# Seven-product pairs in every matrix stage from the output projection to the end of a decoder layer

## The chip, the cores and the metric

The kernel runs on one core of a Trainium2 chip. The metric is the device time of one execution in microseconds; the time of a kernel is the median of its runs. A profile of one execution goes with it; its times count from the first instruction.

## What is computed

One layer of a decoder trunk for 256 tokens of width 2048, all in float32:

```python
h = rmsnorm(x, norm_mix_g)
proj = h @ w_in + b_in                       # 2048 -> 9216, split in six
merged = sigmoid(g_conv) * conformer_conv(u_conv) + sigmoid(g_att) * (moba(q, k, v) @ w_att_out)
x = x + merged @ w_out                       # 2048 -> 2048
h, m = rmsnorm(x, norm_cross_g), rmsnorm(mem, norm_mem_g)
x = x + cross_attention(h, m, w_cq, w_ckv, w_co)   # 4 heads of 512, 256 memory tokens
h = rmsnorm(x, norm_ffn_g)
g, u = split(h @ w_ffn_in)                   # 2048 -> 2 x 5632
x = x + (silu(g) * u) @ w_ffn_out            # 5632 -> 2048
return rmsnorm(x, norm_final_g)
```

The matrices make up nearly all the work: 315 MB of float32 weights, each read once.

## The kernel before

**Products.** Full float32 precision comes from splitting both sides in a high part (a cast to fp32r) and a low part (the rest). A *product* (`mm3`, L214) multiplies a 128 x 128 piece of the left side (features by tokens, stationary) by a 128 x 512 piece of weights in three matmuls: high by high (L217), high by low (L218), low by high (L219). ScalarE makes the high part of the weights, VectorE subtracts it from the raw weights to get the low part; both are recorded under L78, the line of the helper that passes on every operation.

**Blocks.** `stream` (L564) runs a list of blocks, one for each 1024 columns of output and all features: nine for `w_in` (glu, k, q, v, gates), ao0/ao1 and co0/co1 (attention and convolution out), wo0/wo1 (output projection), cq0/1, ck0/1, cv0/1, xo0/1 (cross attention), ffn0 to ffn10 and fo0/fo1. A block has four outputs (token half t, column half n), each in a PSUM bank. Features are taken in pairs of 128. A pair has a kind:

- K: two units of weights of 128 rows each, 128 x 1024 casts; 8 products.
- W: one unit of 256 rows, 128 x 2048 casts; 8 products.
- S: the 2 x 2 product of 128-blocks in seven products (`pair_s`, L507; tables `OF_RAW`, `OF_SUMS`). VectorE makes four sums of the raw weights; unit "a" holds three raw quarters, unit "b" the four sums, and each is cast and subtracted. The left side needs four sums (*forms*) beside its four quarters. The seven products accumulate in their own banks over all S pairs of a block (p1 to p7, with c22 eight in all, the W pairs adding to p2, p3, p4 and c22); `sums_early` (L539) and `result` (L555) put them together with eight adds.

Only ffn1 to ffn10 have S pairs, three of eight (`S_PAIRS`, L1026), and W pairs beside them. All other blocks, ffn0, fo0 and fo1 included, are K. A block of K or W pairs has 64 products (32 in ao and co, 176 in fo), an ffn block with three S pairs 61.

**Order.** The order of the instructions on each engine is written by the program as it is built. In K blocks `advance` (L445) casts and subtracts up to `AHEAD` units before they are used. For W and S units `pump` (L462) does it after each product, when an estimated clock of VectorE or ScalarE is less than `LEAD` ahead of TensorE's (a product counts as 0.68 us). Raw weights land in a ring of half-units (places for 128 rows), high and low parts in another: four places each, ten from `room_for_sums` (L634) in ffn0 on. All weights come by SyncE's (SP's) DMA queue.

Everything else (transposes of a result, the split of the next left side, normalization, attention) is put at a slot so many ticks after the block's evacuation (`at`, L165). Transposes (four 128 x 128 ones in a bank) go to one of two PSUM banks set apart ("misc"); six are for accumulators.

**Left sides.** Each stage has its own 2 MB + 2 MB of high and low parts in SBUF (mg, x2, m, ca, x3, mid); x stays in SBUF until ffn0, where `park_x` writes it to DRAM. The results of the ffn blocks ("mid", 5632 x 256) are transposed and parked in DRAM by ScalarE's queue (L1243). fo0 reloads them pair by pair on SP's queue (`mid_load`, L1257), splits them (`mid_split`, L1263) and keeps all of them for fo1.

Of the kernel before, what the change touches and what calls it, by code (L numbers as in the profile page):

```python
# [37 lines left out]
class Block:  # L38
# [6 lines left out]
    def __init__(self, name, kt, lhs, cols, evac, before=None, kinds=None, forms=None):  # L45
        self.name, self.kt, self.lhs, self.cols, self.evac = name, kt, lhs, cols, evac
        self.before, self.kinds, self.forms = before, kinds or "K" * (kt // 2), forms
# [14 lines left out]
class Timed:  # L62
# [7 lines left out]
    def __getattr__(self, name):  # L70
# [9 lines left out]
        return call  # L80

# [48 lines left out]
class Builder:  # L130
    AHEAD = 6
    LEAD = 0.7

    def __init__(self, ctx, tc, args):
# [16 lines left out]
        self.acc = e(tc.tile_pool(name="acc", bufs=6, space=PSUM))  # L151
        self.misc = e(tc.tile_pool(name="misc", bufs=2, space=PSUM))
# [8 lines left out]
        self.after_sums = []  # L161
# [3 lines left out]
    def at(self, delay, fn, *args):  # L165
        heapq.heappush(self.tasks, (self.slot + delay, self.seq, fn, args))
        self.seq += 1

    def later(self, tr, n):

        for w in range(2):
            self.at(6 + 2 * n + 2 * w, tr, n, w)

    def run_due(self):
        while self.tasks and self.tasks[0][0] <= self.slot:
            _, _, fn, args = heapq.heappop(self.tasks)
            fn(*args)
        self.fill_credit += self.fill_rate
# [4 lines left out]
    def flush(self, upto=None):  # L183
        while self.tasks:
            _, _, fn, args = heapq.heappop(self.tasks)
            fn(*args)
# [21 lines left out]
    def bank(self, shape, name):  # L208
        return self.misc.tile(shape, F32, tag="misc", name=self.nm(name))
# [16 lines left out]
    def transposes(self, src, hi, lo, k, gain=None, mark=None, pool=None):  # L226

        nc = self.nc
        if pool:
            b = pool.tile([P, 2, 2, P], F32, tag="acc", name=self.nm("tr"))  # L230
        else:
            b = self.bank([P, 2, 2, P], "tr")
        for c in range(2):
            for t in range(2):
                nc.tensor.transpose(b[:, c, t, :], src(c, t), self.ident)  # L235
        bb = b.rearrange("p c t s -> p c (t s)")
        if lo is None:
            self.act.copy(hi[:, k : k + 2, :], bb)
        elif gain is None:
            self.split(bb, hi[:, k : k + 2, :], lo[:, k : k + 2, :])  # L240
        else:
            for c in range(2):
                g = self.vecs[:, gain + k + c : gain + k + c + 1]
                self.act.activation(hi[:, k + c, :], bb[:, c, :], AF.Copy, scale=g)
                self.dve.scalar_tensor_tensor(
                    lo[:, k + c, :], bb[:, c, :], g, hi[:, k + c, :].bitcast(F32),
                    op0=ALU.mult, op1=ALU.subtract,
                )
        if mark:
            self.ready.update((mark, k + c) for c in range(2))  # L250

# [18 lines left out]
    def feature_rstd(self, src, first, gap, done):  # L270
# [10 lines left out]
        def total():  # L281
            bk = self.bank([P, 2, 2], "ssq")
# [8 lines left out]
        self.at(first + gap * 7 + 3, total)  # L291

    def rstd_of(self, ss, name):
# [13 lines left out]
        return r  # L307

# [153 lines left out]
    def pump(self):  # L462

        t = self.clock
        while self.n_cast < len(self.units) and self.units[self.n_sub][2] != "K":
            at = self.can_cast()
            if at is not None and max(t["act"], at) < t["pe"] + self.LEAD:
                self.cast_one(at)
                continue
            at = self.can_sub()  # L470
            if at is not None and max(t["dve"], at) < t["pe"] + self.LEAD:
                self.sub_one(at)
                continue
            return

# [4 lines left out]
    def tick(self):  # L480
        self.slot += 1
        self.run_due()

    def acc_of(self, key):
        if key not in self.accs:
            pool = self.misc if key in ("p5", "c22") else self.acc
            self.accs[key] = pool.tile([P, 512], F32, tag="misc" if pool is self.misc else "acc", name=self.nm("acc"))
            self.done[key] = 0
        return self.accs[key]

    def product(self, key, lhs, rhs):
# [6 lines left out]
        t["pe"] += 0.68  # L498
        t["from"] = t["pe"]
        self.pump()  # L500

    def piece(self, blk, k, w, i, t, n):
        lh, ll = blk.lhs(k)
# [3 lines left out]
    def pair_s(self, blk, u, p, first):  # L507

        hi, lo = blk.forms(p)

        self.unit = u

        def go(prods, w):
            for i, (key, left, right) in enumerate(prods):
                f = LEFT[left]
                self.product(key, (hi[:, f, :], lo[:, f, :]), (w[0][:, right, :], w[1][:, right, :]))
# [22 lines left out]
    def sums_early(self):  # L539

        a, dve = self.accs, self.dve
        r = {(t, 1): self.tok_tile([P, 512], "c") for t in range(2)}
        for t in range(2):
            r[t, 0] = self.kept[:, 2 * (self.n_blk % 2) + t]
        self.act.copy(r[0, 0], a["p1"])
        dve.tensor_tensor(r[0, 1], a["p6"], r[0, 0], op=ALU.subtract)
        dve.tensor_tensor(r[1, 0], a["p7"], r[0, 1], op=ALU.add)
        dve.tensor_tensor(r[0, 1], a["p5"], r[0, 1], op=ALU.add)
        dve.tensor_tensor(r[1, 1], a["p5"], r[1, 0], op=ALU.add)
        self.res = r  # L550
        for i, fn in enumerate(self.after_sums):
            self.at(3 + 2 * i, fn)
        self.after_sums = []

    def result(self, blk, t, n):  # L555

# [848 lines left out]
```

## Time and profile before

| | |
|---|---|
| time, median of 3 runs | 1708.89 us (1708.69 to 1710.53) |
| time of the profiled execution | 1708.69 us |
| its span, first to last instruction | 1706.9 us |
| TensorE matmul busy, instructions | 1694.7 us, 7740 |
| VectorE busy | 1186.3 us (70%) |
| ScalarE busy | 854.5 us (50%) |
| GpSimd (POOL) busy | 1.6 us |
| DMA | 346 MB, mean 203 GB/s |

How to read it: matmuls are pipelined, so each is shown longer than the distance between two of them. A row of groups ends with the busy time, the mean of one instruction in ns, the idle time of its engine just before them and who ended it. A row of windows has start and end, the length, and for each engine its busy time and (x) instructions: TensorE's matmuls and weight loads, VectorE (DVE), ScalarE (ACT), GpSimd; then the granted TensorE clock, the busy share of the DMA engines and GB/s.

The blocks that matter start at these times (us): co0 463, wo0 508.5, cq0 599.4, cq1 644.8, ck0 691.1, cv0 782.0, xo0 890.3, ffn0 985.1, ffn1 1030.6, fo0 1455.0, fo1 1576.7.

### The profile page before, as it was taken

Reading aid. Unit: us, or ns where it says so; the run is one execution under the profiler, and the core shown is the slowest. Engines: PE = TensorE matmul, PEld = TensorE weight load, DVE = VectorE, ACT = ScalarE, POOL = GpSimd, SP = SyncE. Lnnn points to the kernel's source line nnn. Section 1 sums busy time; section 2 is a strip of 40 time slices with the busy share of each in tenths; the row PEclk is TensorE's granted clock in tenths of the full one; section 3 lists DMA queues with packets and bytes.
Section 4 is the critical chain, followed back from the end, with each engine's and each line's share of the span. In section 5 each row is a group of like instructions: output and inputs, shape, how many; then the busy total and the mean of one; then the engine's idle time right before and its main releaser. Section 6 shows DMA issues by size and latency. Waiting matters only on the chain.

```text
span 1706.9 us, 20756 instructions
## 1 busy us (share of the span) xinstructions
PE 1694.7 (99%) x7740; PEld 1406.0 (82%) x7740; DVE 1186.3 (70%) x1367; ACT 854.5 (50%) x969; POOL 1.6 (0%) x12
## 2 busy tenths in 40 slices
PE   9999999999999999999999999999999999999998
PEld 7888888888888888888888888888888888888786
DVE  7579987787775566444554569888888887655544
ACT  6444445544544456445444566555555554544433
POOL 0000000000000000000000000000000000000000
PEclk9999999999999999999999999999999999999999
DMA  8665555455666565554355578666666663876653
GB/s 300 197 202 197 198 198 180 158 199 194 209 206 219 186 233 185 185 183 156 131 181 182 184 246 297 213 212 212 211 211 213 210 209 124 315 246 210 194 192 132
DMA packets 129380, 346.00 MB, mean 203 GB/s; under 512 B 14336, under 2 KB 14464, under 8 KB 128896
## 3 DMA queue, kind: packets, MB, share of 16 engines
q1 hardware_dynamic: 125536, 336.12, 59.2%
q10 hardware_dynamic: 3744, 8.56, 1.4%
q8 instruction: 60, 0.98, 0.2%
q14 instruction: 40, 0.33, 0.1%
HBM read 334.67 MB, written 9.96 MB: 202 GB/s over the span
## 4 chain that ended last, share of the span: by engine, by line
PE 98%; ACT 1%; DVE 1%; DMA 0%; issue 0%; ACTq 0%; DVEq 0%
PE acc L218 31%; PE acc L219 31%; PE acc L217 31%; PE tr L235 2%; DVE wlo L78 0%; ACT whi L78 0%; PE cs L219 0%; PE cs L217 0%; PE cb L219 0%; PE cb L218 0%; PE cs L218 0%; PE cb L217 0%; DMA vecs<-in_vecs 0%; PE tr L1048 0%; PE ms L900 0%
## 5 line engine op out<-in xcount | busy, mean ns | idle before, releaser
L78 DVE TENSOR_TENSOR wlo<-raw,whi 128x1024 fp32r<-128x1024 f32 (+2 forms) x474 | 600.2, 1278 | 371.1 <-ACT whi L78 363.8
L78 ACT CAST whi<-raw 128x1024 fp32r<-128x1024 f32 (+2 forms) x474 | 512.8, 1095 | 460.4 <-PE acc L219 362.6
L217 PE MATMUL acc<-whi,xh 128*128 128x512 f32 x576 | 228.9, 397 | 0.7 <-ACT whi L78 0.7
L219 PE MATMUL acc<-whi,xl 128*128 128x512 f32 x576 | 224.6, 390 | 0.0
L218 PE MATMUL acc<-wlo,xh 128*128 128x512 f32 x576 | 224.3, 389 | 0.2 <-DVE wlo L78 0.2
L217 PE MATMUL acc<-whi,x 128*128 128x512 f32 x436 | 171.7, 394 | 0.0
L219 PE MATMUL acc<-whi,x 128*128 128x512 f32 x436 | 170.0, 390 | 0.0
L218 PE MATMUL acc<-wlo,x 128*128 128x512 f32 x436 | 169.8, 389 | 0.0
L217 PE MATMUL acc<-w,x 128*128 128x512 f32 x366 | 143.6, 392 | 0.0
L219 PE MATMUL acc<-w,x 128*128 128x512 f32 x366 | 142.6, 390 | 0.0
L218 PE MATMUL acc<-w,x 128*128 128x512 f32 x366 | 142.5, 389 | 0.0
L218 PE MATMUL acc<-wlo,mid 128*128 128x512 f32 x352 | 137.3, 390 | 1.6 <-DVE wlo L78 1.4
L217 PE MATMUL acc<-whi,mid 128*128 128x512 f32 x352 | 137.3, 390 | 0.1
L219 PE MATMUL acc<-whi,mid 128*128 128x512 f32 x352 | 137.0, 389 | 0.0
L219 PEld LDWEIGHTS acc<-whi,xl 128*128 128x128 f32 x576 | 108.1, 188 | 22.9
L218 PEld LDWEIGHTS acc<-wlo,xh 128*128 128x128 f32 x576 | 108.3, 188 | 22.3 <-DVE wlo L78 0.5
L217 PEld LDWEIGHTS acc<-whi,xh 128*128 128x128 f32 x576 | 108.2, 188 | 22.2 <-ACT whi L78 0.9
L78 DVE TENSOR_TENSOR w<-raw,w 128x2048 fp32r<-128x2048 f32 (+1 forms) x48 | 100.2, 2087 | 16.4 <-DMA raw<-in_w_ffn_in 9.4
L78 DVE SCALAR_TENSOR_TENSOR vy<-vt,vecs,vy 128x256 f32<-128x256 f32 x240 | 104.0, 480 | 0.0
L217 PE MATMUL acc<-whi,m 128*128 128x512 f32 x256 | 101.3, 396 | 0.0
L219 PE MATMUL acc<-whi,m 128*128 128x512 f32 x256 | 99.9, 390 | 0.0
L218 PE MATMUL acc<-wlo,m 128*128 128x512 f32 x256 | 99.7, 390 | 0.0
(219 smaller groups left out, 2476.9 us busy)
## 6 DMA issues: line engine op xcount, KB each, us to landing
raw<-in_w_ffn_in SPq DMA_DIRECT2D x352, 256.0 KB, 4.1
raw<-in_w_in SPq DMA_DIRECT2D x112, 512.0 KB, 4.2
raw<-in_w_ffn_out SPq DMA_DIRECT2D x88, 512.0 KB, 4.7
raw<-in_w_ckv SPq DMA_DIRECT2D x64, 512.0 KB, 3.5
raw<-in_w_in SPq DMA_DIRECT2D x64, 256.0 KB, 4.0
raw<-in_w_out SPq DMA_DIRECT2D x32, 512.0 KB, 4.7
raw<-in_w_cq SPq DMA_DIRECT2D x32, 512.0 KB, 4.6
raw<-in_w_co SPq DMA_DIRECT2D x32, 512.0 KB, 4.0
```

Of the source, the lines that this page charges most:

```text
L78: return f(out, *args, **kwargs)
L217: mm(out, lhs[0], rhs[0], start=start, stop=False)
L218: mm(out, lhs[0], rhs[1], start=False, stop=False)
L219: mm(out, lhs[1], rhs[0], start=False, stop=stop)
L235: nc.tensor.transpose(b[:, c, t, :], src(c, t), self.ident)
```

## The change

1. **S pairs from wo0 on.** Every block from wo0 is made of W and S pairs: two S pairs of eight in wo, cq, ck, cv, xo, ffn0 and ffn1, three in ffn2 to ffn10 as before, six of 22 in fo0 and fo1. ao, co and the blocks before them stay K.
2. **Left sides in shared pieces.** `left_unit` makes one pair's high and low parts, and for an S pair its forms, in 128 x 2048 pieces handed from stage to stage as soon as the last block that reads them has passed (`quad`, `form`, `left_quad_done`). With a gain or an S pair the transposed values are first copied ("a") by ScalarE. As mid's pieces are given back after use, fo1 reloads and splits all of mid again.
3. **Residual in DRAM.** wo and xo load x in 512-column parts into four places ("kept"), add, and write the sum to DRAM; the memory is loaded in eight units through the same places, during cq0 and cq1. These DMAs, mid's stores and reloads go by GpSimd's (POOL's) queue.
4. **Banks by hand.** All eight PSUM banks are one list; accumulators, transposes and attention take whichever was read first.
5. **Work by estimated clocks.** From wo0 on, the pieces of ScalarE's and VectorE's work are tasks with what they depend on and a due time. `pump` emits, after each product and tick, the task or weight operation that can start first (within 0.15 us of it the one due first). Transposes and attention on TensorE wait in a list until what they read is 3 us old by the clocks and a bank is free (`run_aux`).
6. The rings have eight places for parts and six for raw weights from co1 on.

```diff
+                 on_pair=None):
...
-        self.before, self.kinds, self.forms = before, kinds or "K" * (kt // 2), forms
+        self.before, self.last, self.keep, self.on_pair = before, last, keep, on_pair
+        self.kinds = "K" * (kt // 2) if s is None else "".join("WS"[p in s] for p in range(kt // 2))
...
-    LEAD = 0.7
+    LEAD, OLD, PRODUCT = 0.6, 3.0, 0.68
...
-        self.acc = e(tc.tile_pool(name="acc", bufs=6, space=PSUM))
-        self.misc = e(tc.tile_pool(name="misc", bufs=2, space=PSUM))
+        banks = e(tc.tile_pool(name="banks", bufs=1, space=PSUM))
+        self.banks = [banks.tile([P, 512], F32, tag=f"bank{i}", name=f"bank{i}") for i in range(8)]
...
+    def pick(self, eng):
...
+        found = []
+        for x in self.pending[eng]:
+            at = self.start_of(x)
+            if at is not None:
+                found.append((at, x.due, x))
+        if self.n_sub < len(self.units) and self.units[self.n_sub][2] != "K":
+            at = self.can_cast() if eng == "act" else self.can_sub()
+            if at is not None:
+                v = self.n_cast if eng == "act" else self.n_sub
+                due = self.clock["pe"] + (self.products[v] - self.count) * self.PRODUCT - (2.5 if eng == "act" else 0)
+                found.append((max(at, self.clock[eng]), due, self.cast_one if eng == "act" else self.sub_one))
+        if not found:
+            return None
+        first = min(x[0] for x in found)
+        return min((x for x in found if x[0] <= first + 0.15), key=lambda x: x[1])
...
+    def pump(self, until=None):
...
+        until = self.clock["pe"] + self.LEAD if until is None else until
+        while True:
+            found = [x for x in (self.pick(e) for e in ("dve", "act")) if x]
+            if not found:
+                return
+            at, _, x = min(found, key=lambda x: x[0])
+            if at >= until:
+                return
+            if type(x) is Task:
+                self.emit(x)
+            else:
+                x(at)
...
+    def run_aux(self, force=False):
...
+        for i, (fn, deps, when) in enumerate(self.aux):
+            if when and not when():
+                continue
+            if not force:
+                if any(d.done is None or d.done > pe for d in deps):
+                    continue
+                if not any(self.bank_ready(i) <= pe for i in self.free_banks):
+                    return
+            del self.aux[i]
...
+    def left_unit(self, name, p, src, gain=None, at=None):
...
+        first = None
+        if gain is not None or s:
+            first = self.task("act", copy, [], at, due)
+            get = lambda: m["a"]
+        else:
+            get = src
+        high = self.task("act", lambda: act.copy(hi, get()), [first], at, due)
+        low = self.task("dve", lambda: dve.tensor_tensor(lo, get(), hi.bitcast(F32), op=ALU.subtract), [high], at, due)
+        self.marks[name, p] = low
+        if s:
...
+            f = self.task("dve", sums, [first], at, due)
+            h = self.task("act", lambda: act.copy(y[:, 0], m["f"]), [f], at, due)
+            self.marks[name, p, "f"] = self.task(
+                "dve", lambda: dve.tensor_tensor(y[:, 1], m["f"], y[:, 0].bitcast(F32), op=ALU.subtract),
+                [h, low], at, due)
...
-    def room_for_sums(self):
...
+    def more_places(self):
+        for _ in range(2):
+            x = self.big_tile([P, 2, 4, 512], F32R, "w")
+            self.w_ring.add(x[:, 0], x[:, 1])
         x = self.big_tile([P, 8, 512], F32, "raw")
...
+        def load_x(j):
+            for t in range(2):
+                for n in range(2):
+                    c = j * 1024 + n * 512
+                    nc.gpsimd.dma_start(b.kept[:, 2 * t + n], src(t, c))
...
+    S_PAIRS = {"mg": [4, 6], "x2": [4, 6], "m": [5, 6], "ca": [4, 6], "x3": [1, 3, 5], "mid": [3, 6, 9, 12, 15, 18]}
...
+                     S_PAIRS["x3"] if j > 1 else S_PAIRS["x3"][1:], j == 10, True)
...
+    MID_LOADS, MID_SPLITS = 5, 3
...
+    def mid_load(g):
+        p = g % (KF // 2)
+        if g < KF:
+            b.need(b.marks["md", p])
+            m = b.tok_tile([P, 2, S], "mr")
+            nc.gpsimd.dma_start(m, tiles["md"][:, 2 * p : 2 * p + 2, :])
+            mids[g] = m
+    def mid_split(g):
+        j, p = divmod(g, KF // 2)
+        if g < KF:
+            if p == 0:
+                b.left_new(f"mid{j}", S_PAIRS["mid"])
+            m = mids.pop(g)
+            b.left_unit(f"mid{j}", p, lambda: m, None, b.clock["pe"] + 0.5)
...
+        def on_pair(p):
+            g = j * (KF // 2) + p
+            mid_load(g + MID_LOADS)
+            mid_split(g + MID_SPLITS)
...
+        return Block(f"fo{j}", KF, f"mid{j}", [(w, j * 1024), (w, j * 1024 + 512)], evac, before, S_PAIRS["mid"],
+                     True, on_pair=on_pair)
```

More of the change, by code (lines that the diff above doesn't have):

```diff
@@ L224, in split, with transposed @@
         self.dve.tensor_tensor(lo, src, hi.bitcast(F32), op=ALU.subtract)
[L226 to L236, printed above, removed]
+    def transposed(self, src, bank=None):
+        b = self.bank([P, 2, 2, P]) if bank is None else self.view(bank, [P, 2, 2, P])
+        for t in range(2):
+            for c in range(2):
+                self.nc.tensor.transpose(b[:, c, t, :], src(c, t), self.ident)
+        self.clock["pe"] += 0.47
+        return b.rearrange("p c t s -> p c (t s)")
```

862 lines of the change are left out of this document (544 added, 318 removed).

## The prediction

> **What bounds the kernel now.** I read the page first: busy shares, the granted clock over the slices, and the chain that ended last.
>
> ```profile
> span 1706.9 us, 20756 instructions
> PE 1694.7 (99%) x7740; PEld 1406.0 (82%) x7740; DVE 1186.3 (70%) x1367; ACT 854.5 (50%) x969; POOL 1.6 (0%) x12
> PEclk9999999999999999999999999999999999999999
> PE 98%; ACT 1%; DVE 1%; DMA 0%; issue 0%; ACTq 0%; DVEq 0%
> ```
>
> TensorE is busy 99% of the span, at a clock that is never held back, and 98% of the chain is matmuls. As matmuls overlap, a busy share doesn't say how dense they stand. So next the timeline of TensorE, its starts:
>
> ```profile
> 10.21 0.39 PE L218 MATMUL acc<-wlo,xh 128*128 128x512 f32 x1
> ...
> 20.41 0.39 PE L218 MATMUL acc<-wlo,xh 128*128 128x512 f32 x1
> ```
>
> L218 issues one of the three matmuls of every product. These two rows stand 15 products apart: 10.20 / 15 = 0.680 us for a product, whatever the 0.39 us that each matmul is shown with. The matrices' 2370 products (twenty blocks of 64, four of 32, ten of 61, two of 176) then need 1611.6 us, 94% of the span. The rest is transposes, attention, start and tail. The waits of TensorE inside the stream are few:
>
> ```profile
> PE acc L218 <- DVE wlo L78: 1.7, 3, 0.8
> ```
>
> So each product taken away is worth 0.680 us, until another engine becomes late. The only candidate is VectorE. The windows show it by block (wo0, cq0, cq1, ffn1, ffn5, fo0, fo1; the columns that I use are the length, DVE busy, DMA share and GB/s):
>
> ```profile
> 508.50:553.90 45.40, 45.40 (x209) 37.60 (x208) 26.37 (x27) 20.07 (x25) 0.00 (x0) 1.00 0.68 233
> 599.40:644.80 45.40, 45.40 (x210) 37.58 (x208) 26.93 (x36) 27.09 (x39) 0.00 (x0) 1.00 0.68 230
> 644.80:691.10 46.30, 46.30 (x217) 38.50 (x216) 31.02 (x46) 29.42 (x44) 0.00 (x0) 1.00 0.55 184
> 1030.60:1073.00 42.40, 42.40 (x192) 35.11 (x191) 39.65 (x31) 25.11 (x18) 0.00 (x0) 1.00 0.77 266
> 1200.40:1242.80 42.40, 42.40 (x192) 35.09 (x191) 36.98 (x31) 22.44 (x16) 0.00 (x0) 1.00 0.65 211
> 1455.00:1576.70 121.70, 121.02 (x538) 99.83 (x538) 70.34 (x72) 60.77 (x73) 0.00 (x0) 1.00 0.78 266
> 1576.70:1698.60 121.90, 120.93 (x530) 98.92 (x528) 60.59 (x61) 49.21 (x56) 0.00 (x0) 1.00 0.52 170
> ```
>
> VectorE fills 58 to 67% of the blocks that the change turns over, but 87% of an ffn block, which has seven-product pairs already. In ffn1 it fills 39.65 / 42.40 = 93.5%, and TensorE still loses nothing there (61 x 0.680 = 41.5, and its eight transposes). This 93.5% is the highest share that this trace shows to be harmless.
>
> **Products removed.** Each of wo0, wo1, cq0, cq1, ck0, ck1, cv0, cv1, xo0, xo1 gets two pairs of kind S, 64 to 62 products: 20. ffn0 gets two: 2. ffn1 has two where it had three: one more product. fo0 and fo1 get six of 22 each: 12. In sum 33 products x 0.680 = **22.4 us** less on TensorE; the matmuls go from 7740 to 7641. Transposes and attention keep their counts. These 22.4 us lie on the path.
>
> **VectorE's added work.** The rows, each the mean of one instruction:
>
> ```profile
> L78 DVE TENSOR_TENSOR w<-raw,w 128x2048 fp32r<-128x2048 f32 x30 | 68.6, 2288 | 16.4 <-DMA raw<-in_w_ffn_in 9.4 <-ACT w L78 7.0
> L78 DVE TENSOR_TENSOR sums<-raw 128x1024 f32<-128x1024 f32 x30 | 36.6, 1219 | 0.0
> L78 DVE TENSOR_TENSOR sums<-sums,raw 128x512 f32<-128x512 f32 x60 | 41.6, 693 | 2.0
> L78 DVE TENSOR_TENSOR w<-raw,w 128x1536 fp32r<-128x1536 f32 x18 | 31.5, 1752 | 0.0
> L78 DVE TENSOR_TENSOR w<-sums,w 128x2048 fp32r<-128x2048 f32 x18 | 41.2, 2290 | 8.1 <-ACT w L78 8.1
> L78 DVE TENSOR_TENSOR c<-acc,c 128x512 f32<-128x512 f32 x30 | 20.6, 685 | 0.3
> L78 DVE SCALAR_TENSOR_TENSOR raw<-c,ss,raw 128x512 f32<-128x512 f32 x20 | 15.0, 752 | 3.9 <-ACT raw L78 3.9
> L78 DVE TENSOR_TENSOR mid<-mr,mid 128x512 fp32r<-128x512 f32 x22 | 15.1, 686 | 4.8 <-ACT mid L78 4.8
> L78 DVE TENSOR_TENSOR f<-a,f 128x128 f32<-128x128 f32 x6 | 1.8, 292 | 0.2
> L78 DVE TENSOR_TENSOR f<-a 128x256 f32<-128x256 f32 x3 | 1.3, 419 | 0.0
> L78 DVE TENSOR_TENSOR x<-f,x 128x512 fp32r<-128x512 f32 x3 | 2.1, 693 | 2.1 <-ACT x L78 2.1
> ```
>
> A pair of kind W costs 2.288 us. One of kind S costs 1.219 + 2 x 0.693 (sums) + 1.752 + 2.290 (low parts) = 6.65. Putting the seven together costs 8 x 0.685 = 5.48 a block. A left pair costs 0.686 for its low part; in an S pair 0.419 + 2 x 0.292 + 0.693 = 1.70 more. How the sum of such means stands to the busy time: the ffn5 block holds 5 x 2.288 + 3 x 6.65 + 5.48 + 2 x 0.752 = 38.4, and the window shows 36.98, since neighbours overlap. So the factor is 0.964. Now the blocks, against their length less 0.680 for each product saved:
>
> - wo0 and xo1: 6 x 2.288 + 2 x 6.65 + 5.48, four residual adds 2.75, four left pairs of which two S 6.1: 41.4 x 0.964 = 39.9 of 44.0 us. xo0 has the same work in more time.
> - cq0: weights and combining 32.5, the left pairs 4 to 7 of x2 6.1, four units of the memory (a low part and an add of the squares each) 5.5, the reciprocal root about 1: 45.1 x 0.964 = 43.5 of 44.0. **99%.**
> - cq1: 32.5, low parts of q 2.7, four memory units of which two S 5.5 + 3.4: 44.1 x 0.964 = 42.5 of 46.3 - 1.4 = 44.9.
> - fo0 and fo1 (each now reloads and splits all 22 pairs of mid; before, fo1 used fo0's): 16 x 2.288 + 6 x 6.65 + 5.48 + 8 x 0.69 + 22 x 0.686 + 6 x 1.70 = 112.7 x 0.964 = 108.7 of 117.7: 92%.
> - The others stay below 88%: wo1, ck, cv and xo0 have less to do or more time, ffn0 38 of 44.
>
> What hides this is VectorE's idle time, some 10 to 60 us a block before; gone is the cover where the share passes what VectorE can fill. Taking the harmless 93.5% as its bound, cq0 needs 43.5 / 0.935 = 46.5 (+2.5), cq1 45.5 (+0.6), fo0 and fo1 116.3 (0, within their 117.7). I take **+3.1 us**. Below it is 0: the rings let VectorE work ahead. Above it is a lower bound of the share, which is the second rival.
>
> **ScalarE** in fo0: sixteen casts of W, six S pairs, 22 casts of mid and six copies and form casts.
>
> ```profile
> L78 ACT CAST w<-raw 128x2048 fp32r<-128x2048 f32 x30 | 57.4, 1913 | 26.7 <-PE acc L219 16.5 <-DMA raw<-in_w_ffn_in 8.5 <-issue 1.7
> L78 ACT CAST w<-raw 128x1536 fp32r<-128x1536 f32 x18 | 26.6, 1478 | 1.2 <-DMA raw<-in_w_ffn_in 0.7
> L78 ACT CAST w<-sums 128x2048 fp32r<-128x2048 f32 x18 | 34.5, 1915 | 59.3 <-PE acc L219 31.2 <-DVE sums L78 28.0
> L78 ACT CAST x<-a 128x512 fp32r<-128x512 f32 x8 | 5.0, 623 | 0.3
> L78 ACT ACTIVATE a<-tr,vecs 128x256 f32<-128x256 f32 x16 | 6.7, 469 | 5.1 <-PE tr L1048 5.1
> ```
>
> 16 x 1.913 + 6 x 3.39 + 34 x 0.623 + some 4 for the evacuation = 76 us of 117.7. It stays hidden and costs 0.
>
> **Moved DMAs.** Activations, residual, memory and mid go from SP's and ACT's queues to POOL's; SP keeps only weights, so no weight load queues behind a reload any more, and ACT loses its 22 issues.
>
> ```profile
> md<-mid ACTq DMA_DIRECT2D x22, 256.0 KB, 4.7
> mr<-md SPq DMA_DIRECT2D x22, 256.0 KB, 5.2
> ```
>
> (DMA issues, the last column the us to landing; and from the chain of waits one issue on ACT's queue)
>
> ```profile
> 1448.76 0.33 ACTq L1248
> ```
>
> A reload is asked for two pairs, 2 x 8 x 0.68 = 10.9 us, before it is split, and split three pairs before use; that covers 5.2 us. On POOL a store waits for VectorE's add, with the next loads queued behind it; who needs those is an add a block (44 us) later. Traffic in fo0: 266 GB/s x 121.7 / 117.6 = 275; fo1 gains 22 x 256 KB, 170 to about 225. The rings hold less ahead (ten places to eight, raw ten to six in the ffn stage), three pairs or 15 us before a load's data are needed. I take 0. What a DMA of POOL costs this trace doesn't show: from nothing (even a gain of ACT's 22 x 0.33, which nothing waits for) to rival D.
>
> **Tail and seams.** The last block ends with one combining add more before its residual add: +0.7 on the path. Of the present 1.7 us of waits most stand at the seams of fo; the new order may remove or repeat them; I leave them as they are, 0, with -1.7 as the lower end. **Banks:** between the first and the last S pair (pairs 4 to 6) all eight banks accumulate, so a transpose must come before pair 4; a transpose that waits holds every matmul behind it. From the end of a block to pair 4 are 4 x 8 x 0.68 = 21.8 us; I take 0, upper end rival B.
>
> **Sum:** 1706.9 - 22.4 + 3.1 + 0.7 = 1688.3 us of span. This execution took 1708.69 outside its span of 1706.9, 1.8 more; its time is 0.2 below the median of 1708.89. So **1690 us**, 1.1% less. The floor is without VectorE's 3.1 and the old waits: 1685.
>
> **Rivals.** A is the forecast.
>
> B, late left sides: faster, but half the gain is lost. The planner's clocks know durations but not the token buffers, of which eight serve results, copies, forms, squares and reloads. In wo0, cq0, xo0 and ffn0 the block's own S pair uses left sides made in its first 22 us. One unit's chain is 2 x 0.469 + 0.623 + 0.686 = 2.25 us, with forms 2.3 more. Four seams late by one plain unit: +9, **1700**; by an S unit, +18. For it: cq0 at 99%. Against it: the same transposes are finished in time today.
>
> C, VectorE becomes the bound and the kernel is slower: where small dependent tasks mix with casts it can't fill more than the 87% of ffn5. Then cq0 43.5 / 0.87 = 50.0 (+6.0), cq1 +4.0, wo0 and xo1 +1.9 each, fo0 and fo1 108.7 / 0.87 = 124.9, +7.2 each: +28.2 in place of 3.1, **1715**. It decides below a share of about 0.88. For it: ffn blocks have a plain rhythm, fo and cq don't. Against it: ffn1's 93.5%.
>
> D, POOL's issuing and VectorE hold one another. fo has 39 reloads, 8 residual loads and one gain: 48 issues. At ACT's 0.33 us each, 16 us, the slack of 2 x 9 us covers them. At 1 us, taken as three such issues, 48 - 18 = +30, **1720**; it decides from 0.8 us on. For it: nothing in this trace, POOL is idle.
>
> ```profile
> L78 DVE TENSOR_SCALAR o<-o,fsq 128x512 f32<-128x512 f32 x4 | 1.8, 481 | 0.0
> ```
>
> Against it: 512 columns take 481 ns here and 693 in the two-input adds; only such one-input work runs in the faster mode, and fo's weights have none of it.
> The Trainium skill (SBUF — State Buffer, "Who interferes with whom") says that GpSimd writes descriptors through a port pair that VectorE locks in its two-port modes, and that a two-input tensor_tensor has no such mode. By that rule the adds of this kernel hold up no descriptors and D adds nothing; a warning on the same page, that a DMA issued by GpSimd starves behind VectorE, is what would make D true. I lower D from 8 to 4% for it. By the skill's DMA: Bandwidth & Descriptors ("Anatomy of one DMA"), 2.0 us and 436 GB/s, a reload of 256 KB would land in 2.6 us, an estimate; no run here shows it.
>
> E, it saves nothing because the pairs aren't turned over where it says: the instruction count would stay at 7740, **1709**. Only the list of kinds speaks, and it is explicit.
>
> **Chances.** A 0.68, B 0.16, C 0.09, D 0.04, E 0.03. A's own range is 1685 to 1696. Faster by over 0.2% (below 1705.5; 0.2% is about what this kernel's measurement tells from no change): A and B, 0.84. Same: E and a bad B, 0.04. Slower: C and D with a little of B, 0.12. The range from 1684 to 1705 leaves out C, D, E and the worst of B.
>
> **What would show it.** 7641 matmuls; wo to xo blocks shorter by 1.36 us, fo blocks by 4. VectorE at 92% in fo and 95 to 99% in cq, with TensorE's waits there under 4 us. Waits of TensorE for left sides at the fifth pair of a block would be B; VectorE busy below 90% with TensorE waiting for low parts, C; long gaps on VectorE beside POOL's issues, D. I am wrong if the waits on TensorE pass 10 us, or if the product's 0.680 us changes.

## The result and the profile after

| | before | after |
|---|---|---|
| time, us, median (lowest to highest) | 1708.99 (1708.69 to 1710.53), 4 runs | 1688.99 (1687.25 to 1689.48), 4 runs |
| profiled execution, time / span, us | 1708.69 / 1706.9 | 1687.25 / 1685.0 |

The ratio of the times is 0.9879, 95% interval 0.9862 to 0.9896: 1.2% faster. The forecast of 1690 is 1.0 us above the median. In the span the kernel lost 21.9 us; the prediction had 18.6.

From the page of the kernel after, its head and the chain by engine:

```profile
span 1685.0 us, 20850 instructions
PE 1671.7 (99%) x7641; PEld 1387.6 (82%) x7641; DVE 1405.2 (83%) x1557; ACT 926.6 (55%) x957; POOL 63.4 (4%) x127
PE 97%; DVE 1%; DMA 1%; ACT 1%; issue 0%; SPq 0%; DVEq 0%; ACTq 0%
```

Exactly the 7641 matmuls that were predicted. VectorE has 219 us more work and TensorE still makes 97% of the chain, so the added work lies beside the matmuls. The windows by block of the kernel after (wo0, cq0, ck0, xo0, ffn1, ffn5, fo0, fo1; columns as before):

```profile
508.60:552.60 44.00, 44.00 (x203) 36.45 (x202) 38.26 (x37) 23.20 (x19) 0.00 (x0) 1.00 0.61 194
596.70:640.80 44.10, 44.10 (x204) 36.50 (x203) 41.59 (x52) 35.00 (x48) 4.86 (x9) 1.00 0.73 240
684.80:729.70 44.90, 44.90 (x211) 37.35 (x210) 41.98 (x50) 28.57 (x31) 2.14 (x4) 1.00 0.63 216
879.80:929.20 49.40, 48.59 (x235) 40.55 (x234) 42.45 (x43) 25.66 (x24) 0.00 (x0) 1.00 0.54 173
1017.30:1060.40 43.10, 43.10 (x195) 35.70 (x195) 34.63 (x29) 20.65 (x15) 1.08 (x2) 1.00 0.63 210
1187.70:1230.10 42.40, 42.40 (x192) 35.12 (x191) 37.01 (x31) 22.47 (x16) 1.08 (x2) 1.00 0.64 211
1442.20:1558.80 116.60, 116.60 (x520) 96.53 (x520) 104.32 (x102) 72.53 (x69) 17.60 (x33) 1.00 0.85 283
1558.80:1674.50 115.70, 115.70 (x512) 95.71 (x510) 104.81 (x116) 66.57 (x71) 8.59 (x16) 1.00 0.60 195
```

wo0 went from 45.40 to 44.00 us, the 2 x 0.680 of its two products. ffn5, which the change leaves alone, keeps its length and VectorE's work (37.01 and 36.98). fo0 and fo1 are 5.1 and 6.0 shorter (116.5 and 115.4 us from the first matmul of each to fo1's and to the last, 121.6 and 121.3 before), more than their 6 x 0.680 = 4.08. The first number after the comma, TensorE's busy time, equals the length in all blocks shown but xo0 (49.40 less 48.59). VectorE fills 41.59 / 44.10 = 94% of cq0 and the same of ck0, not the 99% reckoned for cq0: part of the memory units slipped from cq0 and cq1 into ck0, which the prediction had below 88% (of the seven adds of the memory's squares two stand in cq0, three in cq1 and two in ck0). fo is at 90%.

What TensorE waits for after its first matrix has begun, by the waits view of the kernel after (us in total, times, longest):

```profile
PE bank L376 <- DVE c L81: 0.8, 1, 0.8
PE bank L376 <- ACT whi L81: 0.5, 1, 0.5
PE bank L377 <- DVE wlo L81: 0.2, 1, 0.2
```

The two lower ones fall into the first 30 us, ahead of the change. In all the changed stages the view leaves TensorE with one wait, 0.8 us in xo0; the prediction allowed 4 in cq. What it hangs on, and the tail, stand in the chain of the kernel after (start, us, what):

```profile
869.43 2.30 DVE wlo L81
871.75 0.33 SPq L645
...
872.13 5.23 DMA raw<-in_w_co
...
877.52 1.92 ACT whi L81
...
879.46 2.29 DVE wlo L81
881.75 0.61 DVE c L81
...
882.41 0.50 PE bank L376
...
1673.44 0.61 DVE c L81
1674.08 0.70 DVE xr L81
1674.80 0.69 DVE o L81
1675.49 0.61 DVE c L81
```

The rows up to 882: a subtraction frees a place of the raw ring at 871.7, and SP issues the next load into it at once. The weights land at 877.4, their cast and their subtraction follow without a gap, and a combining add ("c") stands behind the subtraction on VectorE; the matmul needs the bank that this add reads. So the wait is a weight that landed late because its place came free late, handed on by VectorE's order. The matmul starts 1.18 us after the one before, where the spacing is 0.23; the view counts 0.8 of that, as it takes the 0.39 us that a matmul is shown with as busy. A shorter wait of the same kind, below what the view lists, costs cv1 0.4 us at 833. The last four rows are the tail: combine, residual add and multiply by the gain for one token half, then the same three for the other.

### The profile page after: what moved, and what is told of

Same layout as the page of the kernel before. It is cut to its first block, busy times and chain, and to the rows that moved or that the text cites. A ratio compares the mean times of both kernels' runs of the same rounds, so it can differ in the third digit from the quotient of the medians.

```text
span 1685.0 us, 20850 instructions
## 1 busy us (share of the span) xinstructions
PE 1671.7 (99%) x7641; PEld 1387.6 (82%) x7641; DVE 1405.2 (83%) x1557; ACT 926.6 (55%) x957; POOL 63.4 (4%) x127
## 4 chain that ended last, share of the span: by engine, by line
PE 97%; DVE 1%; DMA 1%; ACT 1%; issue 0%; SPq 0%; DVEq 0%; ACTq 0%
PE bank L376 31%; PE bank L378 31%; PE bank L377 31%; PE bank L390 2%; DVE wlo L81 0%; DMA raw<-in_w_co 0%; DVE w L81 0%; DMA raw<-in_w_ckv 0%; ACT whi L81 0%; ACT w L81 0%; DMA vecs<-in_vecs 0%; PE bank L1233 0%; PE bank L1260 0%; DVE c L81 0%; DVE xr L81 0%
## 5 line engine op out<-in xcount | busy, mean ns | idle before, releaser
L81 DVE TENSOR_TENSOR wlo<-raw,whi 128x1024 fp32r<-128x1024 f32 (+3 forms) x278 | 421.2, 1527 | 129.4 <-ACT whi L81 122.3
L81 ACT CAST whi<-raw 128x1024 fp32r<-128x1024 f32 (+3 forms) x278 | 358.1, 1298 | 256.8 <-PE bank L378 154.6
L376 PE MATMUL bank<-w,op 128*128 128x512 f32 x870 | 341.8, 393 | 0.8 <-DVE c L81 0.8
L378 PE MATMUL bank<-w,op 128*128 128x512 f32 x870 | 338.9, 390 | 0.0
L377 PE MATMUL bank<-w,op 128*128 128x512 f32 x870 | 338.7, 389 | 0.0
L376 PE MATMUL bank<-whi,op 128*128 128x512 f32 x763 | 299.9, 393 | 0.1
L378 PE MATMUL bank<-whi,op 128*128 128x512 f32 x763 | 297.2, 390 | 0.0
L377 PE MATMUL bank<-wlo,op 128*128 128x512 f32 x763 | 297.1, 389 | 0.0
L376 PE MATMUL bank<-whi,xh 128*128 128x512 f32 x576 | 228.9, 397 | 0.5 <-ACT whi L81 0.5
L378 PE MATMUL bank<-whi,xl 128*128 128x512 f32 x576 | 224.6, 390 | 0.0
L377 PE MATMUL bank<-wlo,xh 128*128 128x512 f32 x576 | 224.3, 389 | 0.2 <-DVE wlo L81 0.2
L378 PEld LDWEIGHTS bank<-w,op 128*128 128x128 f32 x870 | 163.3, 188 | 34.3
L376 PEld LDWEIGHTS bank<-w,op 128*128 128x128 f32 x870 | 163.4, 188 | 34.1 <-DVE c L81 1.2
L377 PEld LDWEIGHTS bank<-w,op 128*128 128x128 f32 x870 | 163.5, 188 | 32.7
L378 PEld LDWEIGHTS bank<-whi,op 128*128 128x128 f32 x763 | 143.2, 188 | 30.2
L376 PEld LDWEIGHTS bank<-whi,op 128*128 128x128 f32 x763 | 143.3, 188 | 29.0 <-DVE c L81 0.5
```

The source lines that it names most:

```text
L81: return f(out, *args, **kwargs)
L376: mm(out, lhs[0], rhs[0], start=start, stop=False)
L377: mm(out, lhs[0], rhs[1], start=False, stop=False)
L378: mm(out, lhs[1], rhs[0], start=False, stop=stop)
```

## The experiments

A time without an interval is that of a single execution; those with an interval were timed beside the kernel before, whose median was 1708.75, 1709.16 and 1709.43 us in the three groups of runs. A block's length is taken from its first matmul to the next block's first, and fo1's to its last. The windows shown are cut at 0.1 us or coarser, the last one past fo1's last matmul, so lengths in the text can differ from theirs by some tenths.

**1. The seven-product pairs of fo alone taken back** (`fo_plain`). `s_mode` switches on the order of work by tasks; the edit keeps it on in blocks of W pairs alone, so that only the pairs change:

```diff
-            self.s_mode = "S" in blk.kinds
+            self.s_mode = "K" not in blk.kinds
...
-    S_PAIRS = {..., "mid": [3, 6, 9, 12, 15, 18]}
+    S_PAIRS = {..., "mid": []}
```

> The changed kernel, but fo0 and fo1 have W pairs alone (no seven-product pairs there). Theory A, each product is worth 0.680 us and VectorE's share of fo (about 90%) costs nothing: both fo blocks have 176 products again and get 4.1 us longer (116.5 and 115.8 to about 120.6 and 119.9), the tail loses its extra add (0.7 to 2 us), so the time rises by 6 to 8 us to about 1696. Rival, VectorE at 90% already takes back part of the gain in fo: the blocks get longer by less than 3 us each and the time stays under 1693.

Measured: 1692.97 us (1692.79 to 1693.1), ratio 0.9905 [0.989, 0.992]; span 1691.3, 6.3 above the kernel after. Its windows of fo0 and fo1:

```profile
1442.10:1562.70 120.60, 120.60 (x537) 99.92 (x536) 68.38 (x50) 56.38 (x49) 17.62 (x33) 1.00 0.79 275
1562.70:1682.50 119.80, 119.80 (x530) 99.13 (x528) 65.91 (x60) 51.95 (x54) 8.59 (x16) 1.00 0.58 190
```

Each block is 4.1 us longer than in the kernel after: the products' whole price, with VectorE at 57 and 55% here and 90% there. And they are still 1.0 and 1.9 us shorter than before the change, with as many products: this part of the gain belongs to the new order of work, not to the pairs. It removes the waits at the seams of fo that the prediction left at 0. The time is below the 1696 us that were expected, and as low as the rival had it (under 1693); the rival's reason, blocks longer by less than 3 us, is not found. The kernel after was profiled in its fastest execution, and the medians, 1688.99 and 1692.97, lie 4.0 us apart where the spans lie 6.3 apart; the last section has a reason for 1.5 us of such differences. The tail, from the start of the last matmul to the end of the span, is 8.9 us, against 8.6 before and 10.6 after: most of the tail's growth goes with fo's pairs.

**2. The pairs from wo to xo taken back** (`cross_plain`), with the same edit of `s_mode`; ffn and fo keep theirs:

```diff
-    S_PAIRS = {"mg": [4, 6], "x2": [4, 6], "m": [5, 6], "ca": [4, 6], ...}
+    S_PAIRS = {"mg": [], "x2": [], "m": [], "ca": [], ...}
```

> The changed kernel, but wo, cq, ck, cv and xo have W pairs alone; ffn and fo keep their seven-product pairs. Theory A: ten blocks longer by 1.36 us, 13.6 us in all; the two waits in cv1 and xo0 (about 1.3 us together) may go or stay: 1701 to 1703. Rival, late left sides and VectorE's 94% in cq0 and ck0 cost something that is only hidden by shorter blocks: less than 11 us, under 1700.

Measured: 1699.12 us (1698.96 to 1700.75), ratio 0.9944 [0.9927, 0.996]; span 1697.5, 12.5 above the kernel after, of the 20 x 0.680 = 13.6 that the products cost. The windows of wo0 and cq0:

```profile
508.70:554.20 45.50, 45.50 (x210) 37.64 (x210) 26.93 (x20) 17.61 (x13) 0.00 (x0) 1.00 0.62 203
599.60:645.00 45.40, 45.40 (x209) 37.60 (x208) 27.62 (x29) 34.15 (x49) 5.40 (x10) 1.00 0.77 243
```

Both have their old lengths again. But cv1 and xo0 together grow by 0.8 us, not by the 2.7 of their products: the 1.9 us that they lose in the kernel after go with the pairs. Of these 1.9, 1.5 stand at the two late weights shown above (0.4 at 833 us, 1.1 at 882); the rest wasn't traced. ffn0 is 0.6 us longer, most of it a new wait of a transpose for VectorE. The time is under the 1701 to 1703 us that were expected, and the rival's "under 1700" has the number but not the reason: nothing of what the shorter blocks save is lost to VectorE or to late left sides outside cv1 and xo0. cq0 gives back its 1.36 us in full, although VectorE goes from 61 to 94% in it: the +2.5 us that the prediction charged to VectorE there isn't paid.

**3. How much can VectorE fill?** (`spare`) Extra multiplies of 128 x 248 numbers, 0.41 us each by their mean, as tasks: 8, 12, 16 and 20 of them in ffn3, ffn5, ffn7 and ffn9, two a pair (44) in fo1.

```diff
+    SPARE = {3: 8, 5: 12, 7: 16, 9: 20}
...
+    def spare(n):
+        for _ in range(n):
+            b.task("dve", lambda: dve.tensor_tensor(..., op=ALU.mult), due=5.0)
...
+            spare(2 if j else 0)
```

> The changed kernel with spare VectorE work that nothing reads: multiplications of 128x248 (about 0.40 us) as tasks, 8 in ffn3, 12 in ffn5, 16 in ffn7, 20 in ffn9 and 44 in fo1. It measures which share VectorE can fill. In an ffn block of 42.42 us with 37.0 of work that makes 40.2 (95%), 41.8 (99%), 43.4 (102%) and 45.0 (106%); in fo1 122.5 of 115.8 (106%). If VectorE can fill all: ffn3 and ffn5 keep 42.4, ffn7 and ffn9 get longer only by what goes over (1 and 2.6 us, part of it pushed into the next block), fo1 by 6 to 7. If 93.5% is the limit: ffn3 43.0, ffn5 44.7, ffn7 46.4, ffn9 48.1, fo1 131. If 87% is the limit: ffn3 46, ffn5 48, ffn9 52, fo1 141.

Measured: 1700.05 us, span 1698.3. Windows of ffn5, ffn6, ffn9, ffn10 and fo1, and two waits of TensorE (us in total, times, longest):

```profile
1187.70:1230.20 42.50, 42.50 (x193) 35.15 (x193) 39.75 (x44) 22.77 (x16) 1.08 (x2) 1.00 0.64 211
1230.20:1275.20 45.00, 42.68 (x192) 35.16 (x191) 37.84 (x30) 21.93 (x15) 1.08 (x2) 1.00 0.62 210
1361.00:1403.40 42.40, 42.40 (x192) 35.12 (x191) 41.12 (x50) 21.00 (x16) 1.08 (x2) 1.00 0.58 193
1403.40:1446.80 43.40, 42.73 (x192) 35.18 (x192) 39.83 (x34) 27.68 (x23) 4.79 (x9) 1.00 0.75 252
1563.40:1685.60 122.20, 119.47 (x512) 94.69 (x510) 118.38 (x156) 67.22 (x72) 8.59 (x16) 1.00 0.56 182
```

```profile
PE bank L376 <- ACT mid L81: 3.7, 3, 2.3
PE bank L377 <- DVE wlo L81: 3.0, 8, 0.6
```

ffn5 and ffn9 keep their length, at 93.5 and 97% of VectorE (ffn7 too, at 96%); but the blocks behind them, which got no extra work, are longer: ffn6 by 2.6 us, ffn8 and ffn10 by 1.0. A full block hands some of its work on and moves what the next one does: 2.3 us of the first wait fall into ffn6 and 0.7 each into ffn8 and ffn10. In these three the first four transposes of mid go 8.8 us after the block's start, against 5.45 in the kernel after, and the copy by ScalarE that frees their bank is late; experiment 4 shows this wait from near. In the long block fo1, where less can be put off, VectorE reaches 118.38 / 122.20 = 96.9% and then sets the length (6.5 us more, as expected if VectorE can fill all): seven of the second row's eight waits, for low parts, are here. Rival C needed a limit below 88% for dependent small tasks among casts. The extra multiplies wait for nothing, so 97% is what VectorE reaches with work at hand; with its own tasks alone, the 94% of cq0 in the kernel after cost nothing either.

**4. The age that a transpose waits for** (`old0`, `old15`, `old6`). The list of transposes lets one go when what it reads, and a bank for it, have been ready for OLD us by the estimated clocks; the kernel has 3.0.

```diff
-    LEAD, OLD, PRODUCT = 0.6, 3.0, 0.68
+    LEAD, OLD, PRODUCT = 0.6, 0.0, 0.68
```

and 1.5 and 6.0 in the two others.

> The changed kernel with OLD = 0 in place of 3.0: transposes and attention are put on TensorE as soon as what they read is done by the estimated clocks, without the 3 us in hand. Theory A, the margin keeps TensorE from waiting: TensorE's waits for results rise from about 1 us to 5 to 20 us, time 1692 to 1707. Rival, the estimates are exact enough and the margin does nothing: waits under 2 us, time within 1 us of 1688.

> The changed kernel with OLD = 1.5 in place of 3.0. Theory A, the margin covers the error of the estimated clocks at the transposes, which is what cost 1.55 us in each ffn block at OLD = 0: with 1.5 these waits are gone or under 0.3 us each, time 1687 to 1693. Rival, the error is larger and the cost falls in proportion: about 0.8 us in each ffn block, about 1700.

> The changed kernel with OLD = 6.0 in place of 3.0: transposes and attention 3 us later. Theory A, the left sides have some microseconds in hand before the pair that reads them: waits of TensorE for left sides rise by 0 to 3 us, time 1687 to 1692. Rival, late left sides: units late at the seams of wo0, cq0, xo0 and ffn0, each 2 to 4.5 us, 1695 to 1706.

Measured: 1712.14 (0.0), 1692.44 (1.5) and 1732.54 us (6.0); spans 1710.1, 1690.5, 1730.4, against 1685.0 at 3.0. At 0.0 and 6.0 the loss is larger than either expectation had it. With 6.0 the fourth lot of transposes of xo1's result (at 1011.4 us) comes after a combined result of ffn0 has gone into the same places (1008.5), so the last pair of x3 holds other values; the amount of work is the same. The longest wait of TensorE with 0.0, and below it with 6.0:

```profile
PE bank L390 <- DVE raw L81: 14.3, 11, 1.5
```

```profile
PE bank L376 <- ACT mid L81: 27.3, 9, 3.5
```

L390 issues the transposes. With 0.0 eleven times one stands in TensorE's order ahead of the moment when VectorE has its input, up to 1.5 us early; ffn2 to ffn10 have 44.05 instead of 42.42 us each. With 1.5 they still lose 0.28 us each. So the estimated clocks run ahead of the chip by more than 1.5 us at places, and the 3 us are the margin for it: without them, the change as a whole would be a loss of 3 us.

With 6.0 the first four transposes of mid go 8.8 us after the start of an ffn block in place of 5.45, the next four 32 to 36 us after them. What the first lot costs, in ffn5 of `old6` (TensorE, ScalarE, then TensorE again and the window of its last rows):

```profile
1214.95 0.60 PE L390 MATMUL bank<-consts,raw 128*128 128x128 f32 x4
1218.53 0.50 PE L376 MATMUL bank<-whi,op 128*128 128x512 f32 x1 [2.98 <-ACT mid L81]
```

```profile
1216.09 1.90 ACT L81 CAST whi<-sums 128x2048 fp32r<-128x2048 f32 x1 [3.49 <-DVE sums L81]
1217.90 0.58 ACT L81 COPY mid<-bank 128x512 f32<-128x512 f32 x1
```

```profile
1220.04 0.63 PE L378 MATMUL bank<-whi,op 128*128 128x512 f32 x1
1220.46 0.63 PE L376 MATMUL bank<-w,op 128*128 128x512 f32 x1
```

```profile
1219.50:1222.90 3.40, 3.40 (x9) 2.63 (x9) 1.04 (x2) 1.90 (x1) 0.00 (x0) 0.50 0.73 258
```

The transposes take a bank that the S pair under way needs next. ScalarE's copy, which frees it, stands behind a cast of weights, and the matmul waits 2.98 us. Then the granted clock falls to 0.50 for 3.4 us, and matmuls follow each other after 0.43 us in place of 0.23. The ffn blocks show both prices: ffn3, ffn7 and ffn10, with the wait alone, take 45.7 us, and ffn4 to ffn6, ffn8 and ffn9, with such a stretch of half clock behind it, 47.3. In the whole span half clock makes up 27 us, at 1.6 us lost for each 3.4 some 13 of the 45 us that 6.0 costs. The kernel after has none between its first matrix and its last.

So what the prediction's paragraph on banks warned of, a transpose that holds the matmuls behind it, is real at both ends: up to 1.5 us for an early one and 3.5 for a late one, and the clock on top. Waits for left sides, rival B proper, stay small even here (with 0.0 twice for VectorE's and twice for ScalarE's part of one, 4.3 us in all; with 6.0 once, 1.6). At 3.0 neither happens.

**5. Fewer raw weights ahead** (`raw4`): the raw ring keeps its four places in place of six from co1 on.

```diff
-        self.raw_ring.add(x[:, 0:4])
```

> The changed kernel with four places for raw weights in place of six (two W pairs in place of three). A load lands about 5 us after its issue, cast and subtraction take 4.2 us more, and TensorE takes a W pair in 5.44 us. Theory A, three pairs were needed and are just enough: with two a place turns over in 9 to 11 us against the 10.9 that TensorE gives, so waits for landing weights appear in the fullest blocks: 1692 to 1730. Rival, two are enough: within 1 us of 1688.

Measured: 1730.05 us, at the upper end of what was expected, span 1728.2. The window of fo0, a wait of TensorE and one of ScalarE:

```profile
1468.60:1593.80 125.20, 120.23 (x519) 97.18 (x518) 104.21 (x104) 71.84 (x69) 17.49 (x33) 0.99 0.77 262
```

```profile
PE bank L377 <- DVE w L81: 8.4, 8, 3.3
ACT whi L81 <- DMA raw<-in_w_ffn_in: 64.7, 36, 4.9
```

One pair fewer costs 43 us of span: ScalarE's casts of this one kind wait for their loads 36 times, up to 4.9 us, and TensorE for what comes of them. Here too the granted clock falls to 0.50 behind some of the waits, for 13.7 us in all, by the price above some 6 of the 43 us. That the shorter rings (eight and six places for ten and ten) cost nothing holds for ffn and fo, where the kernel after has no wait; but there is no pair to spare, and the late weights of cv1 and xo0 hang on a raw place that came free late. Whether two places more would remove them wasn't tried.

**6. The reloads of mid on SP's queue instead of POOL's** (`sp_reload`), **and the kernel after once more** (`again`), timed beside each other:

```diff
-            nc.gpsimd.dma_start(m, tiles["md"][:, 2 * p : 2 * p + 2, :])
+            nc.sync.dma_start(m, tiles["md"][:, 2 * p : 2 * p + 2, :])
```

> The changed kernel with the 44 reloads of mid on SP's queue, as before the change, in place of POOL's. Theory A, moving them was free either way: within 0.5 us of the changed kernel in the same call. Rival 1, on SP a reload that waits for its token buffer holds up the weight loads queued behind it: 2 to 10 us more, in fo. Rival 2, POOL's issues (0.54 us each) disturb VectorE: 1 us or more less.

> The changed kernel once more, to see what differs between its executions (spans of 1685.0 to 1687.2 us so far, the profiled one the shortest). Theory A: the block lengths of the first profile come back within 0.1 us, and what differs is a wait for weights landing late (in cv1 and xo0 there were two, 1.3 us together), up to 2 us in ck to xo or fo. Rival: it is the tail, the last outputs' way to DRAM, 10.5 us in the first profile and up to 12.5 now. Time 1688 to 1689.5.

Measured: 1687.70 us (1686.9 to 1688.65), ratio 0.9873 [0.9858, 0.9887] with SP; 1687.67 (1686.61 to 1689.16), 0.9872 [0.9855, 0.9888] unchanged. Which queue reloads mid makes no difference. What POOL's issues cost, and what VectorE's adds beside them take, the groups of the kernel after show (POOL in the whole span, VectorE in fo):

```profile
L1637 POOL DMA_DIRECT2D mr<-md x44 | 23.6, 537 | 159.1 <-DVE op L81 126.9 <-DVE xr L81 11.1 <-issue 7.3
...
L81 DVE TENSOR_TENSOR w<-raw,w 128x2048 fp32r<-128x2048 f32 x27 | 61.8, 2288 | 14.3 <-ACT w L81 14.3
```

An issue on POOL takes 0.54 us, above ACT's 0.33; but the subtraction beside 44 of them still takes 2288 ns, to the digit what it took before.

**7. Trying for more: one S pair more in wo1 and ffn1, and a later multiply by the gain** (`best`), **and the latter alone** (`tail`):

```diff
-    S_PAIRS = {"mg": [4, 6], ...}
+    S_PAIRS = {"mg": [2, 4, 6], ...}      # wo0 uses [4, 6]
...
-                     S_PAIRS["x3"] if j > 1 else S_PAIRS["x3"][1:], ...
+                     S_PAIRS["x3"] if j else S_PAIRS["x3"][1:], ...
...
-                       [x, None if j else y], due=3.0)
+                       [x, None if j else y], due=9.0 if j else 3.0)
```

> The changed kernel with three edits: wo1 and ffn1 get a third seven-product pair (VectorE 84 and 80% there), and in the last block the multiplication by the final gain is due later, so that the last combining adds go first. Theory A, a product is worth 0.680 us wherever VectorE stays under about 95%: wo1 44.07 to 43.39, ffn1 43.10 to 42.42, tail shorter by about 0.5: 1.9 us under the changed kernel of the same call, about 1687. Rival, the new forms made in co1 and the fuller wo1 push VectorE's work into cq0 (94% already), which then waits 1 us or more: no gain.

> The changed kernel with one edit: in the last block the multiplication by the final gain is due later than the last combining adds and the mean. Theory A: from the last matmul's end to the end of the span 10.5 us become about 9.6 (the edit together with two others gave 9.6), all blocks before as in the changed kernel, time 0.8 us less, 1687 to 1688. Rival: the end is set by the output's way to DRAM, nothing changes.

Measured: `best` 1690.78 us (1689.39 to 1691.1), ratio 0.9889 [0.9874, 0.9904], span 1689.3 with 7635 matmuls, 2.9 more than the span of `again`; about 1687 was expected. Its windows of wo0, wo1 and ffn2, and the two waits that are new:

```profile
510.50:556.90 46.40, 44.46 (x204) 36.42 (x204) 38.75 (x40) 22.75 (x19) 0.00 (x0) 1.00 0.56 182
556.90:600.30 43.40, 43.40 (x201) 35.95 (x200) 40.05 (x34) 28.25 (x32) 4.31 (x8) 1.00 0.74 243
1063.80:1108.00 44.20, 42.72 (x192) 35.17 (x192) 37.04 (x31) 22.02 (x15) 1.08 (x2) 1.00 0.63 212
```

```profile
PE bank L376 <- ACT mid L81: 2.2, 2, 1.5
PE bank L376 <- DVE op L81: 1.9, 1, 1.9
```

wo1 gets its 0.68 shorter (43.39 us). But the forms of pair 2 must be made among wo0's left sides, and wo0 waits 1.9 us for one ("op"). ffn1 is 0.3 longer, not 0.68 shorter, and ffn2 1.7 longer: with an S pair as second pair of ffn1, the first transposes of mid go 8.8 us after the start of both, and the matmuls wait for ScalarE's copy as in experiment 4. What is saved is paid in the same block or a neighbouring one, though not in cq0, where the rival had it. `tail`: 1687.74 us (1686.59 to 1688.06), ratio 0.9872 [0.9855, 0.9888]; from the last matmul's start to the end 9.9 us instead of 10.6, which the times can't tell from the kernel after. No version tried is measurably faster than the change.

## Why the prediction was right, and by what margin

| step of the sum | predicted, us | measured, us | from |
|---|---|---|---|
| 33 products x 0.680 | -22.4 | -22.4 | 7641 matmuls; fo 4.1 each and wo0, cq0 1.4 each against experiments 1 and 2 |
| VectorE in cq0, cq1 | +3.1 | 0 there; +1.9 in cv1 and xo0 | windows; experiment 2 |
| waits at the seams | 0 (to -1.7) | -2.9 | fo0 -1.0, fo1 -1.9: experiment 1 |
| tail | +0.7 | +2.0 | start of the last matmul to the end: 8.6 and 10.6 |
| rings, moved DMAs | 0 | 0 in ffn and fo; 1.5 of the 1.9 above hang on a raw place | chain; experiments 5 and 6 |
| span | -18.6 | -21.9 | the terms add to -21.4; the other 0.5 is spread, under 0.1 a block |

- **Products: right.** Each block that was turned over and kept its other work got shorter by 0.680 us a product, and the two experiments that take the pairs back lose the same again (`cross_plain` all but the 1.9 us of cv1 and xo0). ck1 and cv0 only look otherwise, as attention work moved from the one to the other: 45.45 and 58.95 us became 50.80 twice, -2.8 together, and 4 x 0.680 is 2.7.
- **VectorE's +3.1: mis-sized.** The step "taking the harmless 93.5% as its bound" had two errors. The bound was too low: 94% in cq0 and ck0 cost nothing, and VectorE can reach 97% (experiment 3). And the work was booked to the blocks for which it is due: its order by estimated clocks moved some of the memory's work into ck0. In its place stand 1.9 us in cv1 and xo0, 1.5 of them at weights that land late because VectorE's subtraction frees their places late. One reading on the way was off, without effect on the sum: VectorE fills 50% of fo1 before (60.59 of 121.90), not 58 or more.
- **Seams left at 0: mis-sized.** The lower end of -1.7 took the waits that the view listed; the new order removed 2.9 us from fo alone. The listed idle time falls short of the delay: at 1461.8 us of the kernel before a matmul starts 1.08 us after the one before, 0.85 later than at the usual spacing of 0.23, and the view has 0.7, as it counts the 0.39 us of the matmul before as busy.
- **Tail: mis-sized.** The extra combining add is there (0.7). Not foreseen: a multiply by the gain stands ahead of the last combining add in VectorE's order, which keeps that add waiting for 0.6 us after the last matmul's end; `tail` moves it and gets 0.6 back. Of the rest, some 0.3 is the mean for the final norm, which comes behind the last multiply instead of ahead of the last matmul's end, and 0.3 lies behind the last output's issue.
- **The total, and luck.** VectorE -1.2, seams -2.9, the spread -0.5 and tail +1.3 leave the sum 3.3 us too long in the span. That the median is only 1.0 below the forecast is luck: the profiled execution lies 1.7 below the median of its runs, and 0.5 more than before lies outside the span.
- **Rival B**, late left sides, didn't come true; what experiment 4 calls up from either side is mostly its neighbour, transposes that hold the matmuls behind them, and the kernel after sits between. **C** is refuted by fo at 90% and cq0 at 94% without a wait, and by experiment 3 (97%, not 87%), **E** by the count of matmuls.
- **D** is refuted by the 0.54 us of an issue on POOL (it needed 0.8), by the equal 2288 ns and by `sp_reload`. The rule quoted from the Trainium skill (SBUF — State Buffer, "Who interferes with whom"), that two-input adds lock no port that descriptors need, agrees with this; the warning on the same page of starving DMAs doesn't show. For a reload's landing the kernel after has a row now (DMA issues; last column us):

```profile
mr<-md POOLq DMA_DIRECT2D x44, 256.0 KB, 5.8
```

- 5.8 us on POOL's queue, 0.6 more than on SP's before, and within the 10.9 us that were given for it. The estimate of 2.6 us that the prediction worked out from the Trainium skill (DMA: Bandwidth & Descriptors, "Anatomy of one DMA") is less than half of that. The DMA engines move 283 and 195 GB/s in the windows of fo0 and fo1; whether this traffic is the reason wasn't tested.

## What to carry to other kernels

While one engine runs without a gap, the worth of work taken from it is count times spacing of its instructions, read from two distant rows; this was exact here, and all the error lay in the small terms. VectorE, which prepares work, could be filled to 97% here, but the loss stood in the block after a full one. Where an order is written from estimated clocks, the margin for their error (here 3 us, with 5 and 25 us more span at 1.5 and 0, and 45 at 6) deserves a sweep before any other tuning. And a wait can cost more than its length: behind waits of some 3 us in `old6` the clock was halved for another 3.4.

## What was not expected of the hardware

The span of `again` is 1.4 us longer than that of the same kernel's first profile, and no block but glu0 (1.6 us longer) differs by more than 0.2 us; neither a late weight nor the tail, as was expected, makes the difference. It lies in the first ten microseconds; TensorE's timeline of `again`:

```profile
8.27 0.63 PE L377 MATMUL bank<-wlo,xh 128*128 128x512 f32 x1
8.69 0.63 PE L378 MATMUL bank<-whi,xl 128*128 128x512 f32 x1
...
10.57 0.39 PE L377 MATMUL bank<-wlo,xh 128*128 128x512 f32 x1
```

Until 10.0 us after the start a matmul takes 0.63 us and the next follows after 0.43; then it is 0.39 and 0.23. In the first profile of the same kernel the step comes at 5.0 us, ahead of the first matrix. Matmuls of 0.63 us at a spacing of 0.43 are those that `old6` shows at a granted clock of 0.50, so the clock is at half here too. The windows show it as 1.00, but only because the traces hold no record of the clock ahead of the step: the first one starts at 5.2 us in the first profile and at 10.3 in `again`. `best` and `sp_reload` have the late step (10.4 us by this record), the kernel before and `tail` the early one (4.7 and 6.1). The four executions of `again` have spans of 1684.7, 1684.8, 1686.4 and 1686.4 us; the profiled one with the late step is one of the latter two. So single executions of one kernel can differ by 1.5 us here for a reason that has nothing to do with the edit.

What decides between the two wasn't tested. The records give one hint: the stretches of one clock up to the end of the matmuls last whole multiples of 3.413 us (3.41 and 6.83 in `old6`, 1672.53 = 490 x 3.413 in the kernel after), so the clock changes on a grid of that step, and the grid may lie differently against the start of each execution.
